# Filter spectra made beside other layers: the first pair's moved to two earlier tails, the steps paced

## The chip, the cores and the metric

The kernel runs on one core of one Trainium2 chip. The metric is the device time of one launch in microseconds (us). TensorE (PE) does the matrix products, VectorE (DVE) and ScalarE (ACT) the elementwise work, GpSimd (POOL) small powers, memory sets and one DMA queue, SyncE (SP) the other DMA queue.

## The reference

Two blocks of two layers each work on one sequence of 512 tokens, 1024 wide. The first block's layer (here layer a) has a gated short convolution, a sparse attention and a pooling branch, which are merged and projected. The second block's layer (layer b) has an attention, a Hyena long convolution and a gated linear attention, merged and projected, and is followed by a cross attention and a feed-forward of width 4096. The change concerns the Hyena filters, which depend on weights alone:

```python
def hyena_filter_spectra(z, window, w1, b1, w2, b2, w3, b3, freq):
    h = jnp.sin(freq[0] * (z @ w1 + b1))
    h = jnp.sin(freq[1] * (h @ w2 + b2))
    h = (h @ w3 + b3).reshape(L, HY_ORDER, 2, HY_WIDTH) * window[:, None, None, :]
    fwd, bwd = h[:, :, 0], h[:, :, 1]
    f = jnp.concatenate([fwd, zeros, bwd[1:][::-1]], axis=0)
    f = f / (jnp.sum(jnp.abs(f), axis=0, keepdims=True) + EPS)
    return jnp.fft.rfft(f, axis=0)
```

HY_ORDER is 2 (two filters, the "orders"), HY_WIDTH 512. Layer b number l needs the spectra of pair l (both orders), in its long convolution.

## The kernel before

Everything is float32, and each product is done as three products of split operands (`mm3`, lines 242 to 244: high by high, high by low, low by high). A weight block of 512 rows by 256 columns is loaded by SP into `wr` and split by ACT into `wh` (line 220) and by DVE into `wl` (line 221). `gemm_t` gives the result transposed and its products have 512 columns; `gemm_m`, with which layer b begins, has products of 256 columns. A result chunk of 256 columns stands in two PSUM banks of the pool `mm` (four banks), until an evacuation on ACT and DVE frees them. The pool `sd` (four banks) serves all the rest.

A filter pair is made by a generator, `filter_body`, that is advanced by one step at the end of each 256-column chunk of any `gemm` (`step_background`). A pair has a first part (two sines: the features `hA` and `hB`) and then, for each order, four steps that make the taps (rows r = 0 to 3; lines 1056 to 1070), one that begins the butterflies, sums the absolute values over the tokens (line 1088, a product with ones) and inverts the sum (line 1091), and eight parts (b, i). A part takes two butterfly combinations (lines 1147 to 1161), splits each (lines 220 and 221, `p` tiles), multiplies them by a table of the transform (six products, or nine for the first of b = 0; tile `wt`), scales the result by the inverse sum (line 1102), for i = 0 adds the skip weights (line 1104), and POOL's queue stores it (line 1113, `spec`). The code of a step prepares the operands of the next part after it has scaled the present one. The pool of `p` tiles has six buffers, and a stored tile's buffer is free only when the store has landed.

The engines each have one fixed list of instructions, ordered at build time by program place and priority; weight loads and evacuations have a high priority.

Pair 0 is begun in the second layer a, after its attention, and advances one step per chunk through the pooling branch, the gates and the projection (26 chunks). Pair 1 is begun after the first chunk of the first feed-forward, and advances through its other 31 chunks. 28 advances make a pair.

Of the kernel before, what the change touches and what calls it, by code (L numbers as in the profile page):

```python
# [19 lines left out]
P = 128  # L20
# [111 lines left out]
class Kernel:  # L132
    def __init__(self, ctx, tc, A, out, scratch=None):
        self.ctx, self.tc, self.A, self.out = ctx, tc, A, out
        self.nc = tc.nc
        pool = lambda name, **kw: ctx.enter_context(tc.tile_pool(name=name, **kw))
        self.cst = pool("cst", bufs=1)
        self.wp = pool("wp", bufs=3)
        self.bp = pool("bp", bufs=10)
        self.xp = pool("xp", bufs=9)  # L140
        self.sp = pool("sp", bufs=6)
        self.pp = pool("pp", bufs=6)
        self.dp = pool("dp", bufs=1, space=DRAM)
        self.mm = pool("mm", bufs=4, space=PSUM)
        self.sd = pool("sd", bufs=4, space=PSUM)
        self.n = 0
        self.later = []
        self.background = None
        self.consts()


# [135 lines left out]
    def step_background(self, whole=True):  # L287


        if self.background is not None and (whole or self.halves):  # L290
            if next(self.background, self) is self:
                self.background = None

# [669 lines left out]
        return out  # L963


    def filters(self, l):

        nc, A = self.nc, self.A
        spec = self.dp.tile([2, 4, 3, P, 512], F32, tag=f"spec{l}", name=self.nm("spec"), bufs=1)
        self.background, self.halves = self.filter_steps(l, spec), False  # L970
        next(self.background)
        return spec

    def filter_steps(self, l, spec):
        with self.tc.tile_pool(name=f"fg{l}", bufs=1, reuse_waits="tile") as fp:
            self.hp = fp
            yield from self.filter_body(l, spec, fp)

    def filter_body(self, l, spec, fp):
# [3 lines left out]
        w12 = fp.tile([P, P], F32, tag="w12", name=self.nm("w12"))  # L983
        cols = self.small(8, "hycol", bufs=1)
        nc.gpsimd.dma_start(w12[:33, 0:64], A["hy_w1_2"][l])
        nc.gpsimd.dma_start(w12[:64, 64:128], A["hy_w2_2"][l])
        for i, a in enumerate((A["hy_b1_2"][l], A["hy_b2_2"][l], A["hy_freq_2"][l, 0], A["hy_freq_2"][l, 1])):
            nc.gpsimd.dma_start(cols[:64, i : i + 1], a.rearrange("(p o) -> p o", o=1))
        zp = own("win")
        nc.gpsimd.dma_start(zp[:33], A["c_zpos"])  # L990
        h1 = self.p2()
        h2 = self.p2()
# [30 lines left out]
        nxt = taps_w(0)  # L1023
        for dst, lhs, rhs, i in ((h1, w12[:33, 0:64], zp[:33], 0), (h2, w12[:64, 64:128], h1[:64], 1)):
            ps = self.ps_sd()
            nc.tensor.matmul(ps[:64], lhs, rhs, start=True, stop=True)
            arg, n = self.p2()[:64], self.p2()[:64]
            nc.vector.tensor_scalar(arg, ps[:64], cols[:64, i : i + 1], cols[:64, 2 + i : 3 + i], ALU.add, ALU.mult)
            nc.vector.tensor_scalar(n, arg, 1.0 / (2 * math.pi), 12582912.0, ALU.mult, ALU.add)
            nc.vector.tensor_scalar(n, n, 12582912.0, None, ALU.subtract)  # L1030
            for part in (6.28125, 0.0019350051879882812, 3.0199159819567e-07):
                nc.vector.scalar_tensor_tensor(arg, n, -part, arg, ALU.mult, ALU.add)
            nc.vector.tensor_scalar(arg, arg, 3.1415925, -3.1415925, ALU.min, ALU.max)
            nc.scalar.activation(dst[:64], arg, AF.Sin)
            yield
        hB_ = hB.bitcast(F32)
        nc.gpsimd.memset(hB_[64:P], 0.0)
        nc.gpsimd.memset(hB_[64:65], 1.0)
        nc.gpsimd.memset(hB_[96:97], 1.0)
        nc.vector.tensor_copy(hB[:64], h2[:64])  # L1040
        nc.scalar.copy(hA[:64], h2[:64])
        nc.vector.tensor_tensor(hA[64:P], h2[:64], hA[:64].bitcast(F32), ALU.subtract)
        yield
        e = fp.tile([P, 4, 512], F32, tag="fe", name=self.nm("fe"))
        o = fp.tile([P, 4, 512], F32, tag="fo", name=self.nm("fo"))
        for od in range(2):
            w3 = nxt
            acc = self.p2()
            for r in range(4):
                win = own("win")  # L1050
                nc.gpsimd.dma_start(win, A["c_window"][r * P : (r + 1) * P])
                fs = []
                for dr in range(2):
                    ps = self.ps_sd()
# [38 lines left out]
            for m, (b, i) in enumerate(steps):  # L1093
                tH, tL = tabs[b]
                ps = self.ps_sd()
                for z, (sH, sL) in enumerate(ready):
                    self.mm3(ps, tH[:, i, z], tL[:, i, z], sH, sL, z == 0, z == 1)
                    if b == 0 and i == 0 and z == 0:
                        pn = self.ps_sd()
                        self.mm3(pn[0:1], tH[:, 1, 0, 0:1], tL[:, 1, 0, 0:1], sH, sL, True, True)  # L1100
                f = self.p2()
                nc.vector.tensor_tensor(f, ps, rn, ALU.mult)
                if i == 0:
                    nc.vector.tensor_tensor(f, f, sk, ALU.add)
# [9 lines left out]
                if m == 6 and od == 0:  # L1114
# [139 lines left out]
    def layer_b(self, l, st, spec, next_norm):  # L1254
        self.finish_background()
        nc, A = self.nc, self.A
# [55 lines left out]
        gv = self.big(F32)  # L1312
# [77 lines left out]
        qk = [None] * 4  # L1390
# [14 lines left out]
        with self.tc.tile_pool(name=f"gb{l}", bufs=16, reuse_waits="tile") as self.gp:  # L1405
            self.gemm_t(W, 3840, 32, KD, h, ev_lr)
            b, on = self.gla_begin(l, glr)
            self.gemm_t(W, 2304, 512, KD, h, ev_qk)
            self.background, self.halves = self.gla_steps(l, b, on, qk, gv), True
# [372 lines left out]
    def run(self, stop=None):  # L1782
        A = self.A
        tc = self.tc
        spec = [None, None]

        def fill(l):
            spec[l] = self.filters(l)

        st = self.norm_begin(A["norm_g"][0])  # L1790
        self.load_x(st)
        self.defer(self.late_consts, 1)
        x0 = st
        self.defer(lambda: self.store_x(x0), 3)
        st = self.layer_a(0, st, A["norm_g"][1])
        if stop == "a0":
            return self.dump(st)
        st = self.layer_a(1, st, A["ln_mix_2"][0], lambda: fill(0))
        if stop == "a1":
            return self.dump(st)  # L1800
# [38 lines left out]
```

## Time and profile before

| | us |
|---|---|
| median of 3 runs | 3376.39 (3376.36 to 3377.47) |
| the profiled execution, device time | 3377.46 |
| its span, first to last instruction | 3375.7 |
| PE busy in the span | 3322.7 (98%) |
| DVE busy | 2326.8 (69%) |
| ACT busy | 1484.0 (44%) |
| POOL busy | 301.2 (9%) |

The device time of the profiled execution is 1.8 us over its span. PE's busy time is the union of modelled, overlapping intervals, so it does not tell how fast the products follow each other; for that one counts products in a stretch. All places are given in us from the start of the span. In that run the first layer a ends near 572 and the second near 1169 (the last addition of their residuals, line 914), the first feed-forward has its first evacuation at 1912, and the second layer b begins at 2286.

### The profile page before, as it was taken

The page shows a single profiled execution, that of the slowest core. Times are in us where ns is not written, and L with a number is a line of the kernel's source. Part 1 is how long each engine was busy: PE and PEld are TensorE (multiplying, and loading weights), DVE is VectorE, ACT ScalarE, POOL GpSimd, SP SyncE. Part 2 cuts the span into 40 slices and gives each one's busy share as a digit, 9 for nine tenths or more (in the row PEclk, how much of TensorE's full clock was granted, in tenths as well). Part 3 has the DMA queues.
Part 4 walks back from the last instruction along what each step waited for, and adds up shares of the span by engine and source line. Part 5 has one row for each costly group of instructions (what it writes and reads, how often), then busy time and mean ns, then how long its engine had stood idle before and what let it go on. Part 6 is the DMA issues. An engine that isn't in the chain of part 4 may idle for free. (4 is left out here: it accounts for less than half of the span.)

```text
span 3375.7 us, 44852 instructions
## 1 busy us (share of the span) xinstructions
PE 3322.7 (98%) x16960; PEld 2774.1 (82%) x16960; DVE 2326.8 (69%) x4307; ACT 1484.0 (44%) x2455; POOL 301.2 (9%) x472
## 2 busy tenths in 40 slices
PE   8999999999999999999999999999999999999999
PEld 6888888888777887788888888889778888888887
DVE  7966645976778778778766666866876876653354
ACT  6254433435644356533344443344663334433222
POOL 1000000010111110011011101101000101000000
PEclk9999999999999999999999999999999999999999
DMA  5322334332345432235453434433222655233332
GB/s 138 94 76 75 89 112 130 84 95 69 89 118 153 145 80 74 80 100 172 137 177 96 130 123 126 142 120 99 77 80 68 179 149 173 94 125 95 99 114 88
DMA packets 331096, 376.36 MB, mean 111 GB/s; under 512 B 22558, under 2 KB 296852, under 8 KB 330880
## 3 DMA queue, kind: packets, MB, share of 16 engines
q1 hardware_dynamic: 298496, 294.72, 29.3%
q0 software_dynamic: 32384, 78.78, 8.0%
q8 instruction: 133, 2.18, 0.3%
q14 instruction: 83, 0.68, 0.1%
HBM read 340.93 MB, written 32.51 MB: 111 GB/s over the span
## 5 line engine op out<-in xcount | busy, mean ns | idle before, releaser
L242 PE MATMUL mm<-big,wh 128*128 128x512 f32 (+1 forms) x3496 | 1373.7, 393 | 5.7 <-ACT big L220 2.5
L243 PE MATMUL mm<-big,wh 128*128 128x512 f32 (+1 forms) x3496 | 1370.7, 392 | 2.3 <-DVE big L221 2.3
L244 PE MATMUL mm<-big,wl 128*128 128x512 f32 (+1 forms) x3496 | 1368.6, 392 | 0.0
L220 ACT ACTIVATE wh<-wr 128x1024 fp32r<-128x1024 f32 (+2 forms) x528 | 551.3, 1044 | 740.0 <-PE mm L243 516.7
L221 DVE TENSOR_TENSOR wl<-wr,wh 128x1024 fp32r<-128x1024 f32 (+2 forms) x528 | 635.1, 1203 | 291.7 <-PE mm L244 203.8
L242 PEld LDWEIGHTS mm<-big,wh 128*128 128x128 f32 (+1 forms) x3496 | 656.1, 188 | 150.1 <-ACT big L220 4.4
L243 PEld LDWEIGHTS mm<-big,wh 128*128 128x128 f32 (+1 forms) x3496 | 656.5, 188 | 141.7 <-DVE big L221 5.7
L244 PEld LDWEIGHTS mm<-big,wl 128*128 128x128 f32 (+1 forms) x3496 | 656.1, 188 | 137.1 <-issue 1.0
L242 PE MATMUL mm<-wh,big 128*128 128x256 f32 x1056 | 300.4, 284 | 0.0
L243 PE MATMUL mm<-wl,big 128*128 128x256 f32 x1056 | 299.9, 284 | 0.0
L244 PE MATMUL mm<-wh,big 128*128 128x256 f32 x1056 | 299.2, 283 | 0.0
L243 PEld LDWEIGHTS mm<-wl,big 128*128 128x128 f32 x1056 | 202.2, 191 | 1.1 <-DVE wl L221 0.2
L242 PEld LDWEIGHTS mm<-wh,big 128*128 128x128 f32 x1056 | 202.1, 191 | 0.9
L244 PEld LDWEIGHTS mm<-wh,big 128*128 128x128 f32 x1056 | 202.1, 191 | 0.2
L220 ACT ACTIVATE big<-s 128x512 fp32r<-128x512 f32 (+2 forms) x196 | 99.9, 530 | 150.3 <-DVE s L487 87.1
L221 DVE TENSOR_TENSOR big<-s,big 128x512 fp32r<-128x512 f32 (+2 forms) x196 | 107.3, 568 | 18.7 <-ACT big L220 17.0
L1749 DVE TENSOR_TENSOR s<-s 128x512 f32<-128x512 f32 x64 | 43.7, 688 | 103.2 <-ACT s L1748 103.2
L221 DVE TENSOR_TENSOR pt<-sd,pt 128x512 fp32r<-128x512 f32 (+3 forms) x160 | 87.8, 551 | 23.2 <-ACT pt L220 22.4
L220 ACT ACTIVATE pt<-sd 128x512 fp32r<-128x512 f32 (+3 forms) x160 | 76.8, 489 | 61.4 <-PE sd L307 49.3
L914 DVE TENSOR_TENSOR x<-mm,x 128x512 f32<-128x512 f32 x48 | 33.0, 688 | 76.9 <-PE mm L244 76.9
L307 PE MATMUL sd<-c,p 128*128 128x128 f32 x480 | 80.8, 278 | 2.9 <-DVE sm L565 1.2
L1748 ACT ACTIVATE s<-mm 128x512 f32<-128x512 f32 x64 | 37.5, 590 | 102.2 <-PE mm L244 102.2
(423 smaller groups left out, 3967.9 us busy)
## 6 DMA issues: line engine op xcount, KB each, us to landing
wr<-in_w_in_dram SPq DMA_DIRECT2D x244, 512.0 KB, 3.7
wr<-in_mlp_w_dram SPq DMA_DIRECT2D x128, 512.0 KB, 3.6
res<-x POOLq DMA_DIRECT2D x64, 256.0 KB, 2.9
x<-res POOLq DMA_DIRECT2D x48, 256.0 KB, 3.1
F<-spec SPq DMA_DIRECT2D x36, 256.0 KB, 3.7
wr<-in_w_o_dram SPq DMA_DIRECT2D x16, 512.0 KB, 3.5
wt<-in_c_dftf_dram POOLq DMA_DIRECT2D x32, 256.0 KB, 5.0
spec<-p POOLq DMA_DIRECT2D x32, 256.0 KB, 2.7
```

Of the source, the lines that this page charges most:

```text
L220: nc.scalar.activation(H, src, AF.Copy)
L221: nc.vector.tensor_tensor(L, src, H.bitcast(F32), ALU.subtract)
L242: mm(out, aH, bH, start=first, stop=False, **kw)
L243: mm(out, aH, bL, start=False, stop=False, **kw)
L244: mm(out, aL, bH, start=False, stop=last, **kw)
L307: self.nc.tensor.transpose(dst_ps[: s.shape[-1], i * P : i * P + s.shape[0]], s, self.ident)
L914: self.nc.vector.tensor_tensor(X, ps, X, ALU.add)
L1748: nc.scalar.activation(a, ps, AF.Relu)
L1749: nc.vector.tensor_tensor(a, a, a, ALU.mult)
```

## The change

The pair 0 is split: its first part and order 0 are made in the tail of the first layer a, order 1 in that of the second. The features are stored to DRAM in between (`feats`), which adds two stores and two loads of 256 KB. A pace is added: of 12 chunks, only `pace` advance the generator: 8 in the first layer a, 7 in the second, 6 in the first feed-forward, where pair 1 stays whole. `layer_a(0)` and `mlp` (as before) end with `finish_background`, which makes all the steps that are left. The line numbers of the filter code grow by 15 (line 1102 is 1117, 1161 is 1176, 1088 is 1103, 1113 is 1128), those of the helpers by 1 to 4 (220 to 222 becomes 221 to 223, 242 to 244 becomes 243 to 245).

```diff
+        self.pace, self.chunks = 12, 0
...
         if self.background is not None and (whole or self.halves):
+            self.chunks += 1
+            if self.chunks * self.pace // 12 == (self.chunks - 1) * self.pace // 12:
+                return
             if next(self.background, self) is self:
                 self.background = None
...
-    def filters(self, l):
+    def filters(self, l, ods, pace):
+        if 0 in ods:
+            self.spec = self.dp.tile([2, 4, 3, P, 512], F32, tag=f"spec{l}", name=self.nm("spec"), bufs=1)
+            self.feats = self.dp.tile([2, P, 512], F32R, tag=f"feats{l}", name=self.nm("feats"), bufs=1)
+        self.background, self.halves = self.filter_steps(l, self.spec, ods), False
+        self.pace, self.chunks = pace, 0
         next(self.background)
...
+            if len(ods) == 1:
+                for i, t in enumerate((hA, hB)):
+                    nc.gpsimd.dma_start(self.feats[i], t)
+        else:
+            for i, t in enumerate((hA, hB)):
+                nc.gpsimd.dma_start(t, self.feats[i])
+            yield
...
-        for od in range(2):
+        for od in ods:
...
-        st = self.layer_a(0, st, A["norm_g"][1])
+        st = self.layer_a(0, st, A["norm_g"][1], lambda: fill(0, (0,), 8))
+        self.finish_background()
...
-        st = self.layer_a(1, st, A["ln_mix_2"][0], lambda: fill(0))
+        st = self.layer_a(1, st, A["ln_mix_2"][0], lambda: fill(0, (1,), 7))
...
-            st = self.mlp(l, st, *((A["ln_mix_2"][1], lambda: fill(1)) if l == 0 else (None,)))
+            st = self.mlp(l, st, *((A["ln_mix_2"][1], lambda: fill(1, (0, 1), 6)) if l == 0 else (None,)))
```

How it moves instructions is shown at two places. The first is PE's list in the second layer a, at the product with ones that ends the sum of absolute values (`c` is the tile of ones, `p` the sum); before, it stands inside a gemm's second half:

```order
L242 MATMUL mm_9078<-big_4771,wh_9111 128x512
L243 MATMUL mm_9078<-big_4773,wh_9111 128x512
L244 MATMUL mm_9078<-big_4771,wl_9112 128x512
L1088 MATMUL sd_9007<-p_1511_8633,c_83 128x512
L242 MATMUL mm_9079<-big_4771,wh_9111 128x512
```

and now, one order later, at the border of two gemms:

```order
L243 MATMUL mm_9361<-big_5136,wh_9393 128x512
L244 MATMUL mm_9361<-big_5138,wh_9393 128x512
L245 MATMUL mm_9361<-big_5136,wl_9394 128x512
L1103 MATMUL sd_9444<-p_1602_8849,c_83 128x512
L243 MATMUL mm_9452<-big_8694,wh_9455 128x512
L244 MATMUL mm_9452<-big_8695,wh_9455 128x512
```

The product moved from between two products of one chunk to the end of a chunk, with fewer filter steps in the same stretch.

The second place is the start of the second layer b, just behind the first feed-forward. Before, PE has there the narrow products of layer b alone, and among them the four small products that begin its norm (`nsq`); all parts of pair 1 stand ahead, inside the feed-forward:

```order
L242 MATMUL mm_20534<-wh_20590,big_20182 128x256
L243 MATMUL mm_20534<-wl_20591,big_20182 128x256
L244 MATMUL mm_20534<-wh_20590,big_20184 128x256
L342 MATMUL sd_20643<-c_83,nsq_20254 128x1 x4
L242 MATMUL mm_20705<-wh_20708,big_20181 128x256
L243 MATMUL mm_20705<-wl_20709,big_20181 128x256
```

Now PE's list has 192 narrow products of layer b with the last taps of order 1 between them, and then the eight parts of order 1 with nothing but the norm's small products between; shown are the end of the narrow products and the first parts, then the last part:

```order
L245 MATMUL mm_20720<-wh_20776,big_19844 128x256
L244 MATMUL sd_20332<-p_3734_20325,wt_20282 128x512
L245 MATMUL sd_20332<-p_3733_20324,wt_20283 128x512
L243 MATMUL sd_20359<-p_3741_20349,wt_20282 128x512
L244 MATMUL sd_20359<-p_3742_20350,wt_20282 128x512
L245 MATMUL sd_20359<-p_3741_20349,wt_20283 128x512
L243 MATMUL sd_20359<-p_3744_20355,wt_20282 128x512
L244 MATMUL sd_20359<-p_3745_20356,wt_20282 128x512
L245 MATMUL sd_20359<-p_3744_20355,wt_20283 128x512
L243 MATMUL sd_20381<-p_3749_20371,wt_20343 128x512
```

```order
L243 MATMUL sd_20510<-p_3794_20502,wt_20451 128x512
L346 MATMUL sd_20657<-c_83,nsq_19959 128x1 x4
L244 MATMUL sd_20510<-p_3795_20503,wt_20451 128x512
L245 MATMUL sd_20510<-p_3794_20502,wt_20452 128x512
L243 MATMUL sd_20510<-p_3796_20506,wt_20451 128x512
L244 MATMUL sd_20510<-p_3797_20507,wt_20451 128x512
L245 MATMUL sd_20510<-p_3796_20506,wt_20452 128x512
L243 MATMUL mm_20871<-wh_20874,big_19841 128x256
```

So 48 products of pair 1 and the norm's start have moved behind layer b's first 192 narrow products. On DVE's list the same parts now follow each other like this (`p_3737`, `p_3747` and `p_3755` are the scaled results of three parts, `fe` and `fo` hold the butterflies' inputs, `sk` the skip weights):

```order
L1117 TENSOR_TENSOR p_3737_20339<-sd_20332,p_3680_20124 128x512
L1176 SCALAR_TENSOR_TENSOR p_3740_20347<-fo_18081 128x512
L1119 TENSOR_TENSOR p_3737_20339<-p_3737_20339,sk_20306 128x512
L222 TENSOR_TENSOR p_3742_20350<-p_3740_20347,p_3741_20349 128x512
L1176 SCALAR_TENSOR_TENSOR p_3743_20353<-fo_18081 128x512
L222 TENSOR_TENSOR p_3745_20356<-p_3743_20353,p_3744_20355 128x512
L1117 TENSOR_TENSOR p_3747_20366<-sd_20359,p_3680_20124 128x512
L1176 SCALAR_TENSOR_TENSOR p_3748_20369<-fe_18080 128x512
L222 TENSOR_TENSOR p_3750_20372<-p_3748_20369,p_3749_20371 128x512
L1176 SCALAR_TENSOR_TENSOR p_3751_20375<-fe_18080 128x512
L222 TENSOR_TENSOR p_3753_20378<-p_3751_20375,p_3752_20377 128x512
L1117 TENSOR_TENSOR p_3755_20388<-sd_20381,p_3680_20124 128x512
```

Before, each such part had the feed-forward's evacuations and weight splits between its rows; here nothing stands between, and the scaling of a part (L1117) stands ahead of the butterflies of the next.

## Rows read from the trace of the kernel before

**Rows 1.** The page's first part: busy us (share of the span) xinstructions.
```profile
PE 3322.7 (98%) x16960; PEld 2774.1 (82%) x16960; DVE 2326.8 (69%) x4307; ACT 1484.0 (44%) x2455; POOL 301.2 (9%) x472
```

**Rows 2.** Windows: tail with pair 0, next layer's entry, feed-forward, second layer b's start.
```profile
core 0: us, PE busy (x) PEld busy (x) DVE busy (x) ACT busy (x) POOL busy (x), PEclk, DMA share, GB/s
921.00:1125.00 204.00, 196.23 (x827) 154.82 (x826) 167.24 (x237) 87.95 (x123) 31.65 (x60) 0.98 0.46 138
1125.00:1180.00 55.00, 55.00 (x280) 46.51 (x279) 43.62 (x74) 22.72 (x34) 8.70 (x17) 1.00 0.47 147
1920.00:2285.80 365.80, 365.80 (x1601) 299.31 (x1600) 256.21 (x361) 143.82 (x202) 35.39 (x66) 1.00 0.41 127
2286.00:2310.00 24.00, 24.00 (x203) 24.00 (x203) 16.03 (x45) 9.36 (x19) 4.12 (x5) 1.00 0.34 99
```

**Rows 3.** Waits of PE, 921 to 1125: us in total, times, longest.
```profile
PE sd L1088 <- DVE p L1067: 3.3, 1, 3.3
PE sd L243 <- DVE p L221: 2.9, 2, 2.1
PE sd L1056 <- DVE hA L1042: 1.3, 1, 1.3
PE sd L1026 <- ACT p L1034: 0.3, 1, 0.3
```

**Rows 4.** Windows behind the two long waits, columns as in rows 2.
```profile
976.50:979.90 3.40, 3.40 (x8) 2.32 (x7) 3.40 (x6) 1.71 (x3) 0.00 (x0) 0.50 0.45 150
...
1116.50:1119.90 3.40, 3.36 (x8) 2.69 (x9) 3.40 (x5) 0.63 (x1) 0.00 (x0) 0.50 0.11 24
```

**Rows 5.** Timeline 1105 to 1120, one part: start us, us, engine, line [idle before, releaser].
```profile
1106.58 0.69 DVE L221 TENSOR_TENSOR p<-p,p 128x512 fp32r<-128x512 f32 x1 [3.13 <-DMA spec<-p]
1107.19 1.22 DVE L221 TENSOR_TENSOR wl<-wr,wh 128x1024 fp32r<-128x1024 f32 x1
1107.33 0.50 PE L243 MATMUL sd<-p,wt 128*128 128x512 f32 x1 [0.83 <-DVE p L221]
...
1108.32 0.68 DVE L1102 TENSOR_TENSOR p<-sd,p 128x512 f32<-128x512 f32 x1
1108.92 0.68 DVE L1161 SCALAR_TENSOR_TENSOR p<-fe 128x512 f32<-128x512 f32 x1
1109.30 0.55 POOL L1113 DMA_DIRECT2D spec<-p  x1
1109.70 0.63 ACT L220 ACTIVATE p<-p 128x512 fp32r<-128x512 f32 x1 [2.75 <-DVE p L1161]
1110.37 0.69 DVE L221 TENSOR_TENSOR p<-p,p 128x512 fp32r<-128x512 f32 x1 [0.76 <-ACT p L220]
1110.97 0.69 DVE L1161 SCALAR_TENSOR_TENSOR p<-fe 128x512 f32<-128x512 f32 x1
1111.75 0.63 ACT L220 ACTIVATE p<-p 128x512 fp32r<-128x512 f32 x1 [1.42 <-DVE p L1161]
...
1115.79 0.69 DVE L221 TENSOR_TENSOR p<-p,p 128x512 fp32r<-128x512 f32 x1 [4.13 <-DMA spec<-p]
```

**Rows 6.** Lines on DVE, 921 to 1125: busy us, mean ns | idle before, releasers.
```profile
L1059 DVE TENSOR_TENSOR p<-sd,win 128x512 f32<-128x512 f32 x16 | 10.6, 686 | 5.1 <-DMA win<-in_c_window_dram 4.9 <-PE sd L1057 0.2
...
L1091 DVE RECIPROCAL p<-p 128x512 f32<-128x512 f32 x2 | 6.7, 3350 | 0.0
```

**Rows 7.** DMA issues of the stores over the whole run: KB each, median us to landing.
```profile
spec<-p POOLq DMA_DIRECT2D x32, 256.0 KB, 2.7
```

**Rows 8.** Tile `spec`, 1095 to 1125: the same for the three stores there.
```profile
DMA to landing us min/median/max: 2.7/4.0/6.4
```

**Rows 9.** Timeline 2296 to 2316: from the norm's sums to the first evacuation of layer b.
```profile
2297.34 0.95 PE L342 MATMUL sd<-c,nsq 128*128 128x1 f32 x8
...
2298.94 1.03 POOL L351 TENSOR_TENSOR rstd<-ms,c 128x4 f32<-128x4 f32 x1 [7.50 <-DVE ms L350]
...
2300.66 1.00 POOL L533 TENSOR_TENSOR sgk<-sgk,c 128x4 f32<-128x4 f32 x1 [0.68 <-DVE sgk L532]
...
2301.89 0.42 DVE L1303 TENSOR_TENSOR s<-mm,sgk 128x256 f32<-128x256 f32 x1
...
2304.16 0.34 DVE L224 SCALAR_TENSOR_TENSOR big<-mm,rstd,big 128x128 fp32r<-128x128 f32 x1
```

More of the change, by code (lines that the diff above doesn't have):

```diff
@@ L963, in index, with filter_steps, filter_body @@
         return out
-    def filters(self, l):
-        nc, A = self.nc, self.A
-        spec = self.dp.tile([2, 4, 3, P, 512], F32, tag=f"spec{l}", name=self.nm("spec"), bufs=1)
-        self.background, self.halves = self.filter_steps(l, spec), False
+    def filters(self, l, ods, pace):
[4 more added lines that the diff above has]
+        self.pace, self.chunks = pace, 0
         next(self.background)
-        return spec
-    def filter_steps(self, l, spec):
-        with self.tc.tile_pool(name=f"fg{l}", bufs=1, reuse_waits="tile") as fp:
+        return self.spec
+    def filter_steps(self, l, spec, ods):
+        with self.tc.tile_pool(name=f"fg{l}{ods[0]}", bufs=1, reuse_waits="tile") as fp:
             self.hp = fp
-            yield from self.filter_body(l, spec, fp)
-    def filter_body(self, l, spec, fp):
+            yield from self.filter_body(l, spec, fp, ods)
+    def filter_body(self, l, spec, fp, ods):
         nc, A = self.nc, self.A
         own = lambda tag, bufs=1: fp.tile([P, 512], F32, tag=tag, name=self.nm(tag), bufs=bufs)
[L983 to L992, printed above, removed]
         hA = fp.tile([P, 512], F32R, tag="hA", name=self.nm("hA"))
@@ L1021, in table @@
             return [x.rearrange("p (i z f) -> p i z f", i=2, z=2) for x in t]
[L1023 to L1034, printed above, removed]
-            yield
@@ L1036, in filter_body @@
[L1036 to L1043, printed above, removed]
+        nxt = taps_w(ods[0])
+        if ods[0] == 0:
+            w12 = fp.tile([P, P], F32, tag="w12", name=self.nm("w12"))
+            cols = self.small(8, "hycol", bufs=1)
+            nc.gpsimd.dma_start(w12[:33, 0:64], A["hy_w1_2"][l])
+            nc.gpsimd.dma_start(w12[:64, 64:128], A["hy_w2_2"][l])
+            for i, a in enumerate((A["hy_b1_2"][l], A["hy_b2_2"][l], A["hy_freq_2"][l, 0], A["hy_freq_2"][l, 1])):
+                nc.gpsimd.dma_start(cols[:64, i : i + 1], a.rearrange("(p o) -> p o", o=1))
+            zp = own("win")
+            nc.gpsimd.dma_start(zp[:33], A["c_zpos"])
+            h1 = self.p2()
+            h2 = self.p2()
+            for dst, lhs, rhs, i in ((h1, w12[:33, 0:64], zp[:33], 0), (h2, w12[:64, 64:128], h1[:64], 1)):
+                ps = self.ps_sd()
+                nc.tensor.matmul(ps[:64], lhs, rhs, start=True, stop=True)
+                arg, n = self.p2()[:64], self.p2()[:64]
+                nc.vector.tensor_scalar(arg, ps[:64], cols[:64, i : i + 1], cols[:64, 2 + i : 3 + i], ALU.add, ALU.mult)
+                nc.vector.tensor_scalar(n, arg, 1.0 / (2 * math.pi), 12582912.0, ALU.mult, ALU.add)
+                nc.vector.tensor_scalar(n, n, 12582912.0, None, ALU.subtract)
+                for part in (6.28125, 0.0019350051879882812, 3.0199159819567e-07):
+                    nc.vector.scalar_tensor_tensor(arg, n, -part, arg, ALU.mult, ALU.add)
+                nc.vector.tensor_scalar(arg, arg, 3.1415925, -3.1415925, ALU.min, ALU.max)
+                nc.scalar.activation(dst[:64], arg, AF.Sin)
+                yield
+            hB_ = hB.bitcast(F32)
+            nc.gpsimd.memset(hB_[64:P], 0.0)
+            nc.gpsimd.memset(hB_[64:65], 1.0)
+            nc.gpsimd.memset(hB_[96:97], 1.0)
+            nc.vector.tensor_copy(hB[:64], h2[:64])
+            nc.scalar.copy(hA[:64], h2[:64])
+            nc.vector.tensor_tensor(hA[64:P], h2[:64], hA[:64].bitcast(F32), ALU.subtract)
+            yield
+            if len(ods) == 1:
[4 more added lines that the diff above has]
+                nc.gpsimd.dma_start(t, self.feats[i])
+            yield
@@ L1113, in filter_body @@
                 nc.gpsimd.dma_start(spec[od, b, i], f)
-                if m == 6 and od == 0:
+                if m == 6 and od != ods[-1]:
                     nxt = taps_w(1)
@@ L1408, in layer_b @@
             self.gemm_t(W, 2304, 512, KD, h, ev_qk)
-            self.background, self.halves = self.gla_steps(l, b, on, qk, gv), True
+            self.background, self.halves, self.pace = self.gla_steps(l, b, on, qk, gv), True, 12
             self.gate_out(W, 3872, h, A["w_br_attn_2"][l], ya, M, True, None)
@@ L1785, in run, with fill @@
         spec = [None, None]
-        def fill(l):
-            spec[l] = self.filters(l)
+        def fill(l, ods, pace):
+            spec[l] = self.filters(l, ods, pace)
         st = self.norm_begin(A["norm_g"][0])
```

## The prediction, made before the changed kernel had run

> **What bounds the kernel now.** I read the page's busy times first [rows 1]: PE is busy 98% of the span, DVE 69%. Both kernels give PE the same products, so the change can only move the time in which PE waits, or in which it runs at half clock. Then the windows of the stages that make filters [rows 2]. In the feed-forward, pair 1 costs PE nothing: no idle time in 365.8 us, and 1601 products follow each other every 0.2285 us. In the second layer a's tail, 827 products take 204 us, where 827 x 0.2285 would be 189: 15.0 us are lost, of which 204 - 196.23 = 7.8 are idle. The narrow products of layer b follow each other every 24 / 203 = 0.118 us.
>
> The waits of PE in that tail are four kinds, 7.8 us together [rows 3]: the sum of absolute values, the second half of a split, and twice the features. Behind the two long waits the granted clock stood at 0.50, 1.2 GHz, for 3.4 us each [rows 4]; half of that, 3.4 us in all, is lost.
>
> **What the change takes away.** DVE is 82% busy in that tail (167.24 of 204), with one step per chunk. Two thirds and seven twelfths of the steps per chunk leave it room, and the product with ones now stands at the end of a chunk. I take away the waits and the clock behind them, 7.8 + 3.4 = 11.2 us. The bounds are 7.8 (only the idle time) and 15.0 (everything over the feed-forward's pace). The wait for the features, 1.3 + 0.3 [rows 3], has its place in the first layer a now, since that first part is made in the same order there: 1.6 come back. Net gain 9.6. The two stores and two loads of the features stand on POOL's queue between stages hundreds of us apart and cost nothing; were they late, the second tail's first taps would wait some 3 us. The entry of layer b loses its filter steps, but PE idles nowhere in 1125 to 1180 [rows 2]: 0. So does the feed-forward with half the steps per chunk: 0, because nothing was lost there.
>
> **What it adds.** Pair 1 needs 28 advances. It gets one at the start and 31 x 6 / 12 = 15 in the feed-forward; 12 are left for the end, among them all eight parts of order 1. The order shows where they land: three tap steps among layer b's first 192 narrow products, and then eight parts, 48 products, with nothing between. An engine takes its list in order, so PE must wait out the chain of each part.
>
> I count from the end of the feed-forward's last product. *Up to the first part:* DVE has 42 rows from the evacuation of that chunk to the second split of the first part: one inversion of 3.35 us [rows 6], five weight splits of 1.13 (1107.19 to 1108.32) and 36 rows that follow each other in 0.60 (1108.32 to 1108.92) [rows 5], 30.6 us. The last of them starts at 30.0, PE sees it 0.75 later (1106.58 to 1107.33), and I add 1 us for waits on ACT: 31.8. PE's own work up to there is 16 filter products (3.7), the product with ones (0.9, taken as four others) and 192 narrow ones (22.7), 27.3 us. PE waits 4.5.
>
> *One part after the other:* the chain is in the rows of one part [rows 5]. From scaling to butterfly 0.60, to ACT's split 0.78, to DVE's split 0.67, to the second butterfly 0.60, to ACT 0.78, to DVE's second split 0.67 as before, to PE 0.75, through two products to the next scaling 0.99 (1107.33 to 1108.32): 5.85 us. The skip addition fits in the wait on ACT. Three successions are of this kind (17.6). For b = 0 three combinations come before one pair of splits: 0.60 x 3 + 0.78 + 0.67 + 0.63 + 0.75 + 0.99 = 5.6, and 7.4 where three more rows (two of them for the one-row product) stand ahead. For b = 2 one combination: 4.4, and 3.4 + 0.5 to the end of the last product. Sum 38.9. The last product ends at 31.8 + 1.0 + 38.9 = 71.7, and PE's own work to there is 27.3 + 48 x 0.2285 = 38.3. **33.4 us are lost.**
>
> *The stores:* the trace shows a second split waiting for the store of the part before, 3.13 and 4.13 us [rows 5]. Stores land in a median of 2.7 us [rows 7], though in 4.0 and 6.4 at that place [rows 8], behind other transfers. With six buffers and nothing between, a result is stored about one us after its scaling, and its buffer is wanted again a part or so later. Least 0; most, if every part waits as the one in rows 5 did (scaling 1108.32, split 1115.79, then 0.75 + 0.99 = 9.2 us a part), 7 x 3.35 = 23.5. Few other transfers are due there, so I take 2. In the Trainium skill, the page DMA: Bandwidth & Descriptors (Anatomy of one DMA — SWDGE (gpsimd) path) gives about 2.0 us plus the bytes at 436 GB/s, an estimate of 2.6 us for 256 KB; the median agrees, the 6.4 us does not, and by it the stores would cost nothing here and the time be 3411.5.
>
> *The norm and the banks:* layer b's four `mm` banks are full before the parts, and are freed only by evacuations that need the norm. The norm's four products now stand inside the last part. From there to the bank's release were 2304.16 + 0.34 - 2297.34 = 7.2 us, with two powers on POOL [rows 9]; eight small table rows now stand in between, some 0.8; 2.4 pass before the last product ends. PE waits 5.6 more, where the narrow products hid all of it before. The second bank pair comes by the same chain; 48 narrow products (5.7 us) cover most of it: 2, between 0 and 5.
>
> *The clock:* PE works a quarter of the time in this stretch. A wait of 2.1 us was followed by 1.2 GHz, one of 0.83 was not [rows 3, 4, 5]. In a part two products lie on the chain, 0.45 us more at half clock, at most 3.6 in eight parts; I take 2, and 1.7 for one stretch of half clock after the stall, as in rows 4. The Trainium skill (Perfetto Trace Analysis, Matmul Optimizations) says that PE's power follows its utilization, so products should be issued back to back; these are not, and by that rule all eight parts run at half clock and the time is 3415.
>
> Sum of the loss: 33.4 + 2 + 5.6 + 2 + 3.7 = 46.7. **Net +37.1.** The profiled execution took 3377.46, so 3414.6; the median lies 1.1 below it: **3413.5 us**, 1.1% slower.
>
> **Rivals.**
> - *The stores bind.* For it: both waits of rows 5; against: the median of rows 7. Price 21.5 more: 3435.
> - *The chain's hops are covered*, so that DVE's rows alone count: 30.6 + 41 x 0.60 = 55.2 to the last split, 1.2 to the end, less 38.3: 18 lost, and 5.6 for the norm. With the gain at 15.0, +9: 3385. Against it: every second row of DVE's list needs ACT's half first.
> - *The tails keep their waits*, because what delays the taps is the load of their window, for which DVE waited 4.9 us there [rows 6], and not DVE's own time: 9.6 more, 3423.
> - *Faster: the narrow products cover the parts.* If each part's operands are ready when PE comes to it, within its own six products (1.4 us), only the norm's 5.6 is paid against a gain of up to 15.0: 3367. It decides at a part's length: under about 2 us each it is faster, and DVE's five rows a part alone take 3.0. Against it also speaks the order, with no narrow product between the parts.
>
> **How the numbers follow.** Forecast 0.75 (3401 to 3427 by the bounds of the clock, the second banks and the gain), stores 0.12, hops covered 0.06, tails unchanged 0.04, faster 0.03. From the stores' 3435 and the short chain's 3385 I leave out the ends: 3396 to 3434. About 0.2%, 7 us, is what a measurement of this kernel can tell from no change. Faster 0.03; within 0.2% 0.03 (the short chain at its cheapest); slower 0.94.
>
> **What would show it.** In the changed kernel's profile: PE without waits over 1 us in both tails but for the features; in the feed-forward no loss; from about 2280 some 45 us in which PE is mostly idle, released by DVE's and ACT's splits of `p`, parts 4 to 7.5 us apart, the granted clock partly 0.50; then one wait of about 5 us on layer b's evacuation. Parts 9 us apart, released by the stores, would mean the first rival; parts under 4 us the second. The forecast is wrong if PE waits less than 20 us in that place.

## The result, and the profile after

The changed kernel took 3412.47 us (median of 4 runs, 3411.21 to 3416.25), the kernel before in the runs beside it 3376.93: a ratio of 1.0107, 95% interval 1.0089 to 1.0124. It is 1.1% slower; the forecast was 3413.5, and the measured value lies in the forecast's own range. The execution that was profiled took 3411.21 us, with a span of 3409.4.

The page's first part, as in [rows 1]:

```profile
PE 3336.6 (98%) x16960; PEld 2780.6 (82%) x16960; DVE 2327.0 (68%) x4307; ACT 1485.3 (44%) x2455; POOL 304.6 (9%) x476
```

The instruction counts of PE and DVE are the same as before, and PE is again "98% busy". The page cannot tell where 35 us went; the windows can. The first row is the first layer a's tail, the next three answer to [rows 2], and the last three are the last chunk's surroundings, the heap of left-over parts, and what follows:

```profile
core 0: us, PE busy (x) PEld busy (x) DVE busy (x) ACT busy (x) POOL busy (x), PEclk, DMA share, GB/s
372.00:575.00 203.00, 201.62 (x877) 163.49 (x876) 146.12 (x206) 85.07 (x115) 24.52 (x46) 1.00 0.44 132
921.00:1125.00 204.00, 203.28 (x897) 166.53 (x896) 144.66 (x210) 82.71 (x118) 22.75 (x42) 1.00 0.43 129
1125.00:1180.00 55.00, 55.00 (x332) 49.33 (x331) 32.79 (x75) 20.31 (x32) 8.48 (x13) 1.00 0.44 131
1920.00:2266.00 346.00, 346.00 (x1535) 284.83 (x1533) 207.43 (x274) 127.39 (x176) 27.64 (x52) 1.00 0.40 121
2266.00:2291.00 25.00, 22.05 (x167) 20.55 (x165) 23.63 (x33) 9.68 (x14) 1.92 (x4) 1.00 0.44 126
2291.00:2346.00 55.00, 31.36 (x74) 18.01 (x75) 33.60 (x80) 9.88 (x19) 10.57 (x16) 0.50 0.18 62
2346.00:2400.00 54.00, 51.86 (x357) 47.03 (x357) 41.66 (x101) 31.64 (x59) 7.50 (x5) 1.00 0.28 76
```

In the second layer a's tail PE was idle for 7.8 us before; now for 0.7, and it gets 897 products done where it got 827 (of this layer and the next, with fewer of the filters). The feed-forward with half the steps per chunk is without idle time. And between 2291 and 2346 PE does 74 products in 55 us, at a granted clock of 0.50 (1.2 GHz). The waits of PE between 2260 and 2360 are these three kinds (us in total, times, longest):

```profile
PE sd L243 <- ACT p L221: 19.4, 7, 5.4
PE mm L243 <- DVE big L225: 4.0, 1, 4.0
PE sd L244 <- DVE p L222: 2.9, 1, 2.9
```

The wait of 2.9 is the one for the first part, the seven on ACT's half of a split (L221) are one for each later part, and the 4.0 is layer b's evacuation behind the norm. One succession of parts, in the chain of waits (start us, us, what), from one scaling (L1117) to the next:

```profile
2297.07 0.69 DVE p L1117
2297.77 0.61 DVE p L1176
...
2298.40 0.64 ACT p L221
...
2299.06 0.69 DVE p L222
2299.76 0.61 DVE p L1176
...
2300.47 0.64 ACT p L221
...
2301.15 0.80 PE sd L243
2301.95 0.73 PE sd L244
2302.68 0.44 PE sd L245
...
2303.14 0.69 DVE p L1117
```

That is the chain of the forecast, hop by hop, with no DMA in it: 6.07 us, of which PE's part is 2 us. In the timeline the eight scalings start at 2290.97, 2297.07, 2303.14, 2309.26, 2317.01, 2325.76, 2331.08 and 2338.97.

### The profile page after: what moved, and what is told of

Its sections match the earlier page's. It is cut to its first block, busy times and chain, and to the rows that moved or that the text cites. A ratio compares the mean times of both kernels' runs of the same rounds, so it can differ in the third digit from the quotient of the medians.

```text
span 3409.4 us, 44839 instructions
## 1 busy us (share of the span) xinstructions
PE 3336.6 (98%) x16960; PEld 2780.6 (82%) x16960; DVE 2327.0 (68%) x4307; ACT 1485.3 (44%) x2455; POOL 304.6 (9%) x476
## 4 chain that ended last, share of the span: by engine, by line
PE 57%; DVE 4%; ACT 1%; issue 1%; POOL 0%; DMA 0%; ACTq 0%; DVEq 0%; POOLq 0%
PE mm L243 16%; PE mm L244 16%; PE mm L245 16%; PE sd L243 2%; PE sd L244 2%; PE sd L311 2%; PE sd L245 2%; PE sd L589 1%; DVE wl L222 1%; PE sd L1580 0%; PE sd L1352 0%; PE sd L1353 0%; PE sd L1545 0%; DVE gl L1571 0%; DVE big L1492 0%
## 5 line engine op out<-in xcount | busy, mean ns | idle before, releaser
L221 ACT ACTIVATE wh<-wr 128x1024 fp32r<-128x1024 f32 (+2 forms) x528 | 551.7, 1045 | 776.6 <-PE mm L244 532.7
L221 ACT ACTIVATE big<-s 128x512 fp32r<-128x512 f32 (+2 forms) x196 | 100.0, 530 | 153.5 <-DVE s L491 85.8
L221 ACT ACTIVATE pt<-sd 128x512 fp32r<-128x512 f32 (+3 forms) x160 | 76.7, 489 | 60.1 <-PE sd L311 49.0
```

Of the source, the lines that this page charges most:

```text
L221: nc.scalar.activation(H, src, AF.Copy)
```

## The experiments

Each ratio is against runs of the kernel before on the same chip; the interval is the 95% one.

| run | median us | ratio | interval |
|---|---|---|---|
| the change | 3412.47 | 1.0107 | 1.0089 to 1.0124 |
| 12 of 12 in the feed-forward | 3365.13 | 0.9969 | 0.9956 to 0.9981 |
| the heap alone | 3420.60 | 1.0133 | 1.0119 to 1.0147 |
| the split, no pace | 3377.59 | 1.0005 | 0.9996 to 1.0014 |
| 9 of 12 in the feed-forward | 3373.85 | 0.9993 | 0.9984 to 1.0002 |
| more products in the heap | 3408.52 | 1.0091 | 1.0075 to 1.0106 |
| still more | 3408.59 | 1.0091 | 1.0074 to 1.0108 |
| next part prepared ahead | 3396.83 | 1.0060 | 1.0047 to 1.0073 |
| no low half | 3407.97 | 1.0091 | 1.0077 to 1.0104 |
| ones product a chunk later | 3376.55 | 0.9998 | 0.9990 to 1.0007 |
| split, no pace, two windows | 3368.32 | 0.9977 | 0.9968 to 0.9986 |
| before, two windows | 3369.24 | 0.9981 | 0.9972 to 0.9990 |
| split, paces, 12 of 12, two windows | 3366.35 | 0.9972 | 0.9961 to 0.9983 |

### Taking the two halves of the change apart

The heap taken away, the split and the tails' paces kept (here and below, of a long changed line only the call is shown):

```diff
-lambda: fill(1, (0, 1), 6)
+lambda: fill(1, (0, 1), 12)
```

> The changed kernel with pair 1 at 12 of 12 chunks in the feed-forward, so that no step is left for its end; the split of pair 0 and its paces 8 and 7 stay. Theory (all the loss is made by the steps left over, the tails' waits are gone): PE has no idle time from 2280 to 2350, and the time is that of the kernel before less the tails' gain: 9.6 by the prediction, up to 13.4 by the two traces (15.0 lost in that tail before, 1.6 in all now), so 3363 to 3368. Rival (what the tails saved came back elsewhere): 3374 to 3378. Rival (the slower pace, and not the heap at the end, costs something too): that cost is gone as well, and the time falls below 3360.

It took 3365.13, 10.8 below the 3375.89 of the kernel before. To price the heap in the trace I take one stretch in both kernels: from layer b's first narrow product to the norm's two products behind its 384th (L377). First the changed kernel, then this one, windows as above:

```profile
2260.90:2366.60 105.70, 79.11 (x450) 63.96 (x450) 77.02 (x166) 31.63 (x56) 18.18 (x26) 0.74 0.29 86
```

```profile
2274.40:2321.34 46.94, 46.94 (x393) 46.90 (x393) 30.05 (x82) 17.85 (x33) 7.40 (x7) 1.00 0.34 102
```

58.8 us more. The `sd` products in the stretch are 66 and 8, so 58 of pair 1 stand in it; at the feed-forward's 0.2285, and 0.7 more for the one with ones, they are 14.0 us of PE's own work. The heap loses 44.8 us, and that is all of the loss: the spans of the two profiled executions, 3409.4 and 3364.4, differ by 45.0.

The heap alone: pair 0 whole in the second layer a with a step per chunk, only the feed-forward paced.

```diff
-st = self.layer_a(0, st, A["norm_g"][1], lambda: fill(0, (0,), 8))
-self.finish_background()
+st = self.layer_a(0, st, A["norm_g"][1])
...
-st = self.layer_a(1, st, A["ln_mix_2"][0], lambda: fill(0, (1,), 7))
+st = self.layer_a(1, st, A["ln_mix_2"][0], lambda: fill(0, (0, 1), 12))
```

> The kernel before with one thing of the change, the pace of 6 of 12 in the first feed-forward; pair 0 is whole in the second layer a, one step per chunk. Theory (loss and gain are independent and add up): the heap alone costs what the changed kernel lost plus what the tails gained, 35.5 + 9.6 to 13.4, so 3422 to 3426. Rival (the tails gained nothing, and the heap costs less than its 46.7 forecast): 3412 to 3414.

3420.60, 44.7 above the kernel before on that chip, a little less than expected (3422 to 3426); PE's waits on ACT in the heap are the same 19.4 us in seven. Loss and gain add up: 44.7 - 10.8 = 33.9, measured for both 35.5; the difference of 1.6 is less than these intervals can tell.

Fewer steps left over:

```diff
-lambda: fill(1, (0, 1), 6)
+lambda: fill(1, (0, 1), 9)
```

> The changed kernel with pair 1 at 9 of 12 chunks in the feed-forward: four of its parts are left for the end instead of twelve steps. In PE's list their 27 products stand among layer b's first narrow products, with 65, 66, 31 and 20 of those ahead of or between them, where in the changed kernel the eight parts stood behind 192 narrow ones with nothing between. Theory (what costs is a part whose chain no other product covers): 65 narrow products are 7.7 us and cover a chain of 5.3 to 8.8, 20 to 31 cover 2.4 to 3.7 of it, so the loss is 3 to 6 for the last two parts and at most 5.6 for the norm, against the kernel without any steps left 3 to 12 us: 3367 to 3378. Rival (a part left over costs its chain wherever it stands): 4 parts x 5 us + 6 for the norm = 26, so 3390 to 3393.

3373.85, in the theory's range. The window over the same stretch, and the waits of PE between 2260 and 2345:

```profile
2268.70:2329.20 60.50, 55.96 (x420) 53.49 (x419) 46.17 (x122) 21.35 (x40) 12.20 (x15) 0.97 0.34 104
```

```profile
PE mm L243 <- DVE big L225: 4.1, 1, 4.1
...
```

Four parts stand behind the feed-forward here, and PE waits for none of them; the one long wait left is the norm's 4.1. With 27 products (6.2 us) the stretch is 60.50 - 46.94 - 6.2 = 7.4 us longer, of which 4.5 are PE's idle time (60.50 - 55.96) and some 1.5 the half clock behind the norm's wait. So in this run PE waits for no part's chain: a chain is waited for where no other product stands ahead of it. In the changed kernel the 192 narrow products that the free banks allow were used up ahead of the parts, by the taps.

### What the heap's parts wait for

The next part's operands prepared ahead of the scaling, in the second order of pair 1 alone (cut to its core; the buffers, and one more copy on DVE, are left out here):

```diff
+            late = l == 1 and od == 1
...
+                ahead = late and m + 1 < len(steps)
+                if ahead:
+                    coming = prepare(*steps[m + 1])
                 for z, (sH, sL) in enumerate(ready):
...
-                    ready = prepare(*steps[m + 1])
+                    ready = coming if ahead else prepare(*steps[m + 1])
```

> The changed kernel with pair 1's second order written so that the operands of the next part are prepared ahead of the scaling of the present one; the buffers for it are those of the dead features, window and two of the tables' and one more. In DVE's list half of the parts then have their butterflies ahead of the scaling. Theory (the heap's price is the chain from one part's scaling through butterfly, split and split to its products): where the operands are ready, a part takes its products' 2.6 us at half clock or DVE's five rows of 0.60, so four of the seven successions lose 2 to 3 us, and the time falls by 8 to 14 us: 3398 to 3404. Rival (DVE's rows or the stores' buffers bind, not the order of the chain): 3409 to 3414.

3396.83, some 15 us less than the changed kernel, and 1 us below the theory's range. The waits of PE on split halves in that kernel, 2260 to 2360:

```profile
PE sd L243 <- ACT hA L221: 4.8, 3, 3.2
...
PE sd L243 <- ACT p L221: 2.3, 2, 1.5
PE sd L244 <- DVE hB L222: 1.1, 3, 0.4
```

19.4 us have become 8.2 (4.8 + 2.3 + 1.1) behind the first part. It is the same work, and one copy more, on the same engines in another order: the chain binds, not DVE's rows. The run also gives some tiles buffers of their own, so by itself it does not rule the stores out; the changed kernel does, where no wait of PE or DVE in the heap ended with a store.

DVE's half of the split left out:

```diff
+                if l == 1 and od == 1:
+                    res = []
+                    for a in self.bfly((e, o)[i], b):
+                        H = self.p2(F32R)
+                        nc.scalar.copy(H, a)
+                        res.append((H, H))
+                    return res
                 return self.parts(self.bfly((e, o)[i], b), self.p2)
```

> The changed kernel without DVE's half of the split in pair 1's eight last parts (the high half stands in for the low one, so PE has the same products; that leaves out the low order part of these operands). Sixteen DVE rows of 0.67 us go. Theory (the chain binds): from the scaling to the next scaling now 0.60 + 0.60, ACT's half 0.8, six products at half clock 2.6 and 0.7 behind, 4.9 to 5.3 instead of 6.1, and about 2 us less where b = 0: the time falls by 8 to 14 us, 3398 to 3404. Rival (something off that chain, as the stores, sets the pace): 3410 to 3414.

3407.97: 4 to 5 us less by the medians, half or less of what the theory expected, a little more than the rival, and the two ratios' intervals overlap. Inside the parts the theory came nearer: from the first scaling to the last part's last product it is 39.7 us (2288.88 to 2328.56), where the changed kernel has 46.6 (2290.97 to 2337.6). The three successions of the first kind took 5.02, 3.82 and 4.92 for 6.1, two as expected and the shortest at full clock. Those of the b = 0 parts hardly changed (7.91 and 8.28 for 7.75 and 8.75): in the changed kernel PE waits there for ACT's half alone, and nine and six products follow that wait. And 3.5 us came back behind the parts: the norm's products now stand behind the last part instead of inside it, and the wait for the norm is 6.0 for 4.0:

```profile
PE sd L243 <- ACT p L1103: 20.8, 8, 5.4
PE mm L243 <- DVE big L225: 6.0, 1, 6.0
```

### What the half clock costs

Products that nobody needs, behind each of the first seven parts:

```diff
+                if l == 1 and od == 1 and m < 7:
+                    dm = self.ps_sd()
+                    for _ in range(8):
+                        nc.tensor.matmul(dm, tH[:, i, 1], sL, start=True, stop=True)
                 f = self.p2()
```

> The changed kernel with eight more products of 512 columns behind each of the first seven left-over parts of pair 1, into a bank that nobody reads; they need only operands that the part has used already. In the changed kernel PE idles some 2.2 us between a part's last product and the next part's first; eight products take 1.8 us at 2.4 GHz and 3.4 at 1.2 GHz. Theory (the granted clock of 0.50 comes from PE's idling, and costs only what lies on a part's chain: 2 us in seven parts, some 2 more in the two parts with b = 0, 1.8 behind the stall): the clock comes back to 1.00 inside the heap, parts of the first kind follow each other in 5.8 instead of 6.1 us, and the time falls by 2 to 6 us, to 3407 to 3410. Rival (half clock costs 0.2 us for each of the 74 products in that stretch, 15 us): 3397 to 3400. Rival (the clock stays at 0.50 whatever PE does there): each part is 1.2 us longer, 3419 to 3421.

3408.52, in the theory's range, and far from both rivals. (The first rival's 15 us takes the 21 narrow and the 8 one-column products for wide ones; with 45 at 0.20 and 18.5 narrow ones at 0.096 it is 11, and would give 3401.) The ratio's interval overlaps the changed kernel's, so the trace must tell. The window over the heap (PEclk is the third number from the end), and four of the scalings:

```profile
2291.00:2346.00 55.00, 40.67 (x150) 27.96 (x150) 36.00 (x91) 11.96 (x25) 10.53 (x16) 0.84 0.17 60
```

```profile
2296.66 0.69 DVE L1121 TENSOR_TENSOR p<-sd,p 128x512 f32<-128x512 f32 x1 [1.31 <-PE sd L245]
2302.51 0.69 DVE L1121 TENSOR_TENSOR p<-sd,p 128x512 f32<-128x512 f32 x1 [0.83 <-PE sd L245]
2308.13 0.69 DVE L1121 TENSOR_TENSOR p<-sd,p 128x512 f32<-128x512 f32 x1 [0.82 <-PE sd L245]
2315.79 0.69 DVE L1121 TENSOR_TENSOR p<-sd,p 128x512 f32<-128x512 f32 x1 [2.65 <-PE sd L245]
```

PE does 150 products there for 74, at a mean clock of 0.84 for 0.50, and two parts of the first kind follow in 5.85 and 5.62 us. The part with b = 0 still took 7.66, for the clock fell again there. So the longer gaps got more:

```diff
-                    for _ in range(8):
+                    for _ in range({3: 14, 4: 22}.get(m, 8)):
```

> As the run with eight more products behind a left-over part, but fourteen and twenty-two of them ahead of the two parts with b = 0, where PE idles longest (3.6 and 5.4 us); there the granted clock had still fallen to 0.50, just as the nine products of such a part began. Theory (half clock lies on the chain of those two parts with 1.6 and 1.0 us, six and more products standing behind the last wait): the clock stays at 1.00 through the b = 0 parts, their successions fall from 7.75 and 8.75 us to about 6.0 and 7.4, and the time is 2 to 3 us below that run: ratio to the kernel before 1.0083 to 1.0086, 3404 to 3407. Rival (DVE's and ACT's rows alone set those parts): the successions stay at 7.7 and 8.8, and the ratio at 1.009.

The time did not fall: 3408.59, and the theory's 3404 to 3407 is missed; within its interval that run can't tell 2 us. In the trace the products of the first b = 0 part, all but the first two, ran at full clock:

```profile
2291.00:2346.00 55.00, 44.14 (x173) 31.59 (x174) 36.32 (x90) 11.44 (x24) 10.53 (x16) 0.88 0.19 63
2315.20:2317.10 1.90, 1.86 (x8) 1.35 (x9) 0.69 (x1) 0.00 (x0) 0.00 (x0) 1.00 0.00 0
```

From the first scaling to the last (2292.28 to 2336.66) it is 44.4 us, where the changed kernel has 48.0 and the run with eight products 45.7. Over the longer stretch, from layer b's first narrow product to the norm's two products (L377), the three have 102.9, 105.7 and 104.2. So some 3 us of the heap (3.6 by the first count, 2.9 by the second) were half clock on the chain, less what the extra products cost themselves. The two b = 0 successions fell only to 6.97 and 8.28, not to 6.0 and 7.4; for the first of them the fourteen extra products ran at half clock at first, and the part's own products started right behind their end, at 2314.23.

### Why the tails' waits went

The split with a step in every chunk:

```diff
-fill(0, (0,), 8)
+fill(0, (0,), 12)
...
-fill(0, (1,), 7)
+fill(0, (1,), 12)
...
-fill(1, (0, 1), 6)
+fill(1, (0, 1), 12)
```

> The split of pair 0 alone, all paces 12 of 12. Theory (the room on DVE that the slower pace leaves takes the tails' waits away): with one step per chunk the product with ones and the split halves wait as before, in both tails now, so 3372 to 3379. Rival (the split alone does it, because half the steps make half the waits or because they fall beside other work): 3363 to 3369.

3377.59, as the theory expected: the split alone gives nothing, the pace does. PE waited at the product with ones in both tails. I took the product's place for the reason, and moved it one step on:

```diff
             ready = prepare(*steps[0])
+            yield
             ps = self.ps_sd()
             nc.tensor.matmul(ps, self.ones, acc, start=True, stop=True)
```

> The split with 12 of 12 everywhere, as in the run that had the split without a pace, and one more step between the sum of absolute values and its product with ones, which therefore stands one chunk later in PE's list. In that run PE waited 2.7 and 1.9 us for that product's operand and only 0.5 for a split. Theory (in the tails the place of that one product is what costs; a slower pace helps because the same sum is then ready in time): both waits and the half clock behind them go, 7 to 9 us, so 3368 to 3371. Rival (DVE has no room at one step per chunk, wherever the product stands): 3375 to 3378, with the waits at the product or at the splits.

3376.55: that theory fell. The product stands a chunk later and waits 3.2 and 1.8 us. But DVE is not full: in the chunks up to the first of these waits it is busy 44.87 of 55 us:

```profile
372.00:427.00 55.00, 50.65 (x214) 39.21 (x214) 44.87 (x66) 27.41 (x36) 11.02 (x21) 1.00 0.47 140
```

What DVE waits for just ahead of the sum stands in the waits of the run without a pace, 372 to 430 and 921 to 985, DVE's row and PE's:

```profile
DVE p L1074 <- DMA win<-in_c_window_dram: 4.2, 2, 2.9
...
PE sd L1103 <- DVE p L1082: 2.6, 1, 2.6
...
DVE p L1074 <- DMA win<-in_c_window_dram: 3.7, 2, 2.6
...
PE sd L1103 <- DVE p L1082: 2.0, 1, 2.0
```

The window tile has one buffer, so its next load starts only when the last tap of the row before has been multiplied, and it lands 3.0 to 4.8 us after its issue. A second buffer, first in the split without a pace, then in the kernel before:

```diff
-            w12 = fp.tile([P, P], F32, tag="w12", name=self.nm("w12"))
+            w12 = own("sk")
...
-            zp = own("win")
+            zp = own("win", 2)
...
-                win = own("win")
+                win = own("win", 2)
```

> The split with 12 of 12 everywhere, and a second buffer for the window tile, so that the next window's load need not wait for the present one's last use (the sines' weights move into the skip weights' tile to make the room). In the run with the split alone DVE waited 2.9 and 1.3 us for the window's load in the first layer a's tail, 2.6 and 1.1 in the second's, just ahead of the sum for which PE then waits 2.6 and 2.0 us. Theory (the window's load delays the sum, not DVE's work): those waits end, the sum is ready 3 to 4 us sooner, PE's two waits and the half clock go, and the time is 3367 to 3371. Rival (DVE has no room at one step per chunk): 3375 to 3379, with PE's waits at the product with ones still there.

> The kernel before with that second window buffer and nothing else. Theory (the window's load delays the sum): of the waits of PE in the second layer a the 3.3 us at the product with ones and the half clock behind it go, 5 to 6 us; the 2.9 us at the splits, which stood behind stores, stay: 3369 to 3372. Rival (DVE has no room there): 3375 to 3378.

3368.32 and 3369.24, both in the theory's range. In the first of them PE's waits at the product with ones are 0.3 us and none, for 2.6 and 2.0. The waits of PE from 921 to 1125 in the second of them, which answer to [rows 3]:

```profile
PE sd L243 <- DVE p L221: 2.4, 2, 2.1
PE sd L1056 <- DVE hA L1042: 1.3, 1, 1.3
...
PE sd L1088 <- DVE p L1067: 0.2, 1, 0.2
```

The 3.3 at the product with ones has become 0.2, and DVE's waits for the window, 4.9 us in [rows 6], are gone; the 2.1 at a split, behind a store, stays. DVE's work is unchanged, and the tail's 204 us hold more of it than the 167.24 before, not less, so DVE had the room:

```profile
921.00:1125.00 204.00, 199.85 (x862) 159.69 (x861) 171.60 (x244) 91.67 (x129) 31.47 (x59) 1.00 0.46 141
```

With the pace and the second buffer together:

> The split with paces 8 and 7, 12 of 12 in the feed-forward, and the second window buffer. With the pace DVE waited for a window only 0.2 us, so both theories expect the time of the run with 12 of 12 in the feed-forward, 3363 to 3367.

3366.35: nothing more than the pace gives. By the medians the fastest kernel is the change with 12 of 12 in the feed-forward, 0.3% below the kernel before; one buffer in the kernel before gives 0.2% without splitting anything, and the intervals of these four runs overlap.

## Why the prediction was right, and where its steps were not

The sum came out at +37.1 and was +35.5, with the likeliest case and its mechanism: an engine's list in which nothing stands between the parts of a chain. That the sum came so close is partly luck: the parts cost 3.2 us more than forecast and the loss's other terms together 5.1 less, and the gain came for another reason than the one given. Term by term, forecast to measured:

- **The feed-forward and layer b's entry**, 0 to 0: PE is busy 346.00 of 346.00 us, and 55.00 of 55.00.
- **The gain**, 9.6 to 10.8. The amount was right and the reason was not. "Two thirds and seven twelfths of the steps per chunk leave it room" was the step: DVE had the room before. Its waits for the window made the sum late, and a pace below 12 gives the load its time: in that tail DVE waited 4.9 us for windows [rows 6], and in the changed kernel not at all (first line below). The rival in which the load delays the taps had the cause right, but took from it that a pace would not help. The features' wait came back, 1.2 + 0.2 us for the 1.6 taken.
- **Up to the first part**, 4.5 to 2.9. PE saw the split 31.1 us behind the feed-forward's last product (2259.12, where the product behind it starts, to 2290.21; second and third line below) for the forecast's 31.8, and 28.2 of them were its own work, for 27.3.
- **The parts**, 32.9 with their shares of the stores (2) and the clock (2), to 36.1, which is what the 44.8 leave when the other terms are taken off. Three successions of 5.85 were 6.10, 6.07 and 6.12; at full clock they were 5.85 and 5.62. The step that failed is the b = 0 parts: "0.60 x 3 + 0.78 + 0.67 + 0.63 + 0.75 + 0.99 = 5.6" lets two products follow the last wait, and nine do in the first of these parts, six in the second. 7.75 and 8.75 stand there for 5.6 and 7.4, 5.32 for the next 4.4, and 6.5 (2331.08 to the last product's end at 2337.6) for the last 3.9, where the norm's sums come in between. The sum also takes PE's own work in the parts as 48 products; with the three one-row products they are 51, 0.7 us more.
- **The stores**, 2 to 0: no wait in the heap ends with one, and they land in a median of 2.3 us (last line below). The Trainium skill's price in DMA: Bandwidth & Descriptors (Anatomy of one DMA — SWDGE (gpsimd) path), an estimate of 2.6 us for 256 KB, is 0.3 above that, and its forecast of no cost was right.
- **The norm**, 5.6 to 4.0, **and the second banks**, 2 to 0.
- **The clock**, 3.7 to an estimate of 5.4: the 3.6 of the 36.1 by which the parts shortened when PE had more to do, and 1.8 behind the stall (18.5 narrow products of 0.214 instead of 0.118, 2341.77 to 2345.72). The Trainium skill's rule (Perfetto Trace Analysis, Matmul Optimizations), by which the whole heap runs slow because its products are not back to back, agrees with the changed kernel's 0.50 from 2291 to 2346; the last section has stretches where it does not tell the clock. The slower products took 11 us longer (45 wide ones 0.43 instead of 0.23, and the narrow ones), but by this estimate only 5.4 of that lengthened the stretch, because most of them stand beside a wait.

The lines for these terms, all of the changed kernel:

```profile
L1074 DVE TENSOR_TENSOR p<-sd,win 128x512 f32<-128x512 f32 x8 | 5.3, 684 | 1.0 <-PE sd L1072 1.0
...
2258.88 0.40 PE L245 MATMUL mm<-big,wl 128*128 128x512 f32 x1
...
2290.21 0.50 PE L244 MATMUL sd<-p,wt 128*128 128x512 f32 x1 [2.88 <-DVE p L222]
...
DMA to landing us min/median/max: 2.3/2.3/4.0
```

The other rivals: 9.2 us a part for the stores was not seen, nor parts under 4 us. That narrow products cover the parts, with which the change would have been faster, is what happens with four parts left over instead of eight: there the kernel is as fast as before.

## What to carry to other kernels

Work that hides behind a stream of products is free only while products of that stream stand in front of it in the engine's list: a slower pace cost nothing inside the stream here, and the whole chain for each part that was left with no product ahead of it, so count the advances before setting a pace. When an engine waits for a result that comes late, follow the producer's own waits before blaming its load; here one more buffer for a 256 KB load did, by the medians, two thirds of what splitting and pacing did (7.0 of 10.8 us). And a chain of small operations over three engines is shortened by preparing the next link ahead (15 us here), more than by leaving an operation out (4 to 5, not clear of the noise).

## What was not expected of the hardware

A wait of the same length was followed by different clocks. The forecast read in the kernel before that a wait of 2.1 us was followed by 1.2 GHz. With two windows and nothing else changed, the wait at that split is again 2.07 us, and the products behind it take 0.23 us each, which is 2.4 GHz. First the kernel before, then the run with two windows:

```profile
1116.54 0.80 PE L243 MATMUL sd<-p,wt 128*128 128x512 f32 x1 [2.07 <-DVE p L221]
1117.13 0.63 PE L244 MATMUL sd<-p,wt 128*128 128x512 f32 x1
```

```profile
1110.26 0.50 PE L243 MATMUL sd<-p,wt 128*128 128x512 f32 x1 [2.07 <-DVE p L221]
1110.60 0.40 PE L244 MATMUL sd<-p,wt 128*128 128x512 f32 x1
```

So the 7.0 us that the second buffer gained are more than the wait of 3.1 that went: some 1.7 each, by an estimate, come from the two stretches of half clock of 3.4 us in [rows 4], which are not there in this run. Nor did the granted clock rise and fall with PE's busy time. In the run with the next part prepared ahead, PE was busy 13.76 of 16.8 us and stayed at 0.50:

```profile
2290.60:2307.40 16.80, 13.76 (x26) 7.00 (x26) 13.32 (x22) 3.99 (x7) 4.30 (x8) 0.50 0.41 126
```

In the run without the low half, the clock rose behind six products at half clock and stayed at 1.00 for 6.7 us in which PE was busy for 2.62 and waited twice for 2.2, then fell again:

```profile
2290.70:2294.10 3.40, 2.93 (x6) 1.73 (x6) 0.86 (x3) 0.73 (x2) 0.99 (x2) 0.51 0.56 201
2294.20:2300.90 6.70, 2.62 (x9) 1.54 (x9) 4.09 (x7) 2.40 (x4) 1.63 (x3) 1.00 0.39 117
2301.00:2311.00 10.00, 5.74 (x12) 2.90 (x12) 3.12 (x5) 1.14 (x2) 0.54 (x1) 0.50 0.14 52
```

Busy times at the two clocks are not alike, since a wide product takes 0.43 us at 1.2 GHz and 0.23 at 2.4; counted in products, the first stretch has 26 in 16.8 us and the one at full clock 9 in 6.7. What decides the clock in such stretches stays open; none of these runs was made to tell.
